# HGRN2 and sliding-window trunk on one core: order of casts, copies and turns at six places, and the last tile in column halves

## The chip, the cores and the metric

The kernel runs on one core of a Trainium2 chip. The metric is the time of one execution on the device, in microseconds (us). Before the change the median of three timed runs is 2102.97 us (2102.83 to 2103.01).

## What is computed

The input `x` has 1024 tokens of 1024 features, in float32. Two layers follow, each a token mixer and a gated feed-forward network (FFN), every one of the four sub-layers closed by a layer norm of `ALPHA * h + sublayer(h)`:

```python
# layer 0: HGRN2, 8 heads of 128
q, f, i, g = jnp.split(h @ w_in, 4, axis=-1)                  # w_in: 1024 x 4096
fg = lb + (1.0 - lb) * jax.nn.sigmoid(heads(f))               # lb: softmax over two rows of logits
o = hgrn2_chunkwise(jax.nn.silu(heads(q)), 1.0 - fg, heads(i), jnp.log(fg))
o = o * lax.rsqrt(jnp.mean(jnp.square(o), -1, keepdims=True) + RMS_EPS)
o = o * g_norm_w * jax.nn.silu(heads(g))
mix = o.reshape(B, S, D) @ w_out
# S_t = diag(f_t) S_{t-1} + k_t v_t^T ;  o_t = S_t^T q_t
# layer 1: attention over a window of 128, 16 query heads and 4 shared key/value heads, with sinks and a bias
# each layer's FFN, 1024 -> 2 x 2816 -> 1024:
u = causal_depthwise_conv3(h @ w_in) + conv_b
a, b = jnp.split(u, 2, axis=-1)
ff = (jax.nn.silu(a) * b) @ w_out
h = layer_norm(ALPHA * h + ff, g, b)
```

## The kernel before

**Products.** A float32 product is made of three matmuls of a reduced format, fp32r. Each operand is split into a *high* part, its cast to fp32r, and a *low* part, the operand less its high part. `mm3` (L222 to L224) issues high by high, high by low and low by high into one PSUM bank. `split` (L249) makes both parts: the high one is a cast on ScalarE (ACT), the low one a subtraction on VectorE (DVE) in `low_part` (L197). So each operand passes through ScalarE and then VectorE before TensorE (PE) can finish with it. `T` holds the turned (transposed) activations, features on the partitions: `T[:, 0]` is the high part, `T[:, 1]` the low. `HL` holds the split weights. `psmm` are PSUM tiles of one bank (128 x 512), `psax` PSUM tiles of two banks (128 x 1024).

**What sets the order.** Most of the program is under a manual schedule: each engine executes its instructions in the order in which the Python code emits them, and an object `od` interleaves the emission. `od.t` is a planned time in us that the code of TensorE's products moves on; `od.spawn(task, delay)` and `od.later(delay, call)` put a task aside until the plan has come that far, `yield d` in a task waits for d planned us, `od.behind(x, y)` works out such a wait from how far VectorE's own plan is ahead, and `od.tick()`, called after each k step of three matmuls, emits what is due. A delay therefore only chooses the place in the engines' orders. While the chip runs, an instruction waits for its operands and for whatever stands ahead of it on its engine.

**The beginning.** `x` arrives in eight blocks of 128 tokens in `Y`, and the weights of head 0's values and gates in two pieces, `raw0` and `raw1`, on the SP queue. TensorE first runs matmuls on a zero tile `still`. `x_block(0)` transposes block 0 into two banks, casts them, makes the low parts and copies the rows out to `xf[0]` (the tile `St`, L923). `ig_second` (L840) splits `raw1`; `first_rows` (L851) multiplies blocks 0 and 1 by both pieces. `x_first` turns block 1 (again by `x_block`, its rows go to `qp`) and blocks 2 and 3 (`turn_block`, a `psax` tile; the rows go to `tot` and `og`, L965). In all of them the low part is made from PSUM. `lower_bounds` (`le`, L976 to L978) runs between block 2 and block 3 on ScalarE. `ig_block` (L811 and L812) then multiplies blocks 2 and 3, and blocks 4 to 7 are turned by `x_pair`, which also spawns `sums_of_x`, sums of blocks for the later products by block schemes.

**Head 0.** `first_qf` makes the forget gate and the query of head 0. `forget` makes the gate of a half of the tokens by three activations on ScalarE (L1041, L1045, L1046), which give `fg` and `kp`. `recur` is the recurrence of one head; its first operation on VectorE is `qp = qs * fg` (L1158).

**The other heads.** Their q, f, i and g projections are made by 7-product block schemes (`line` lists them), with `evacuate` taking each product out of PSUM. A head's last value product is followed by `turn_values` (its transposes are in the group L232, the copy back is L1254, the waited-for copy L1421). `norm` closes a head: squares, a scale on VectorE (L1275), the transposes of `og`, and for the last head the split of the result into `T`. The results of heads 0 to 6 come back and are split into `T` by `move`, which puts the low parts into the list `moved_lows`; `lay`, called while ticking, takes from it what is due, and `lay_all` the rest. The out-projection `out_pass` (L1574) reads them.

**FFN.** `Up.run` multiplies by a 7-product scheme: column block after column block (`fc`) of two weight columns. Its first products, before all blocks of the normed activations are there, are run in parts: of product 1, for fc 0 and 1, the columns of three token blocks first, then `make` finishes the sums (`TX`, `rx`), then the fourth, 128 columns wide. `collect` takes products out of PSUM: product 1 is copied twice by ScalarE (L522, L523), the others are added by VectorE. `Down` runs seven products, the last of which is number 4, and `evacuate` (L691) adds each bank to `Y`. After product 4's tile `tb` follow `ln_half` (statistics of 512 columns, L263), then `ln_affine`: `ln_stats` aggregates (L269, L270, and a power on GpSimd), two passes scale (L280, L283), and the rows leave on the SP queue.

Of the kernel before, what the change touches and what calls it, by code (L numbers as in the profile page):

```python
# [134 lines left out]
def trunk(ctx: ExitStack, tc: tile.TileContext, a: dict, out: bass.AP):  # L135
# [120 lines left out]

    half_stats = {}

    def ln_half(tb, i):

        if tb not in half_stats:
            half_stats[tb] = sm.tile([P, 2, 6], F32, name="st", bufs=8)
        nc.vector.bn_stats(half_stats[tb][:, i, :], Y[:, tb, i * 512:(i + 1) * 512])  # L263

    def ln_stats(tb):
        st = half_stats.pop(tb)
# [28 lines left out]
    def quarters(to, rows):  # L295
# [110 lines left out]
    class Up:  # L406
# [93 lines left out]
            split(blocks(1, 0), blocks(1, 1), r1)  # L500
            split(blocks(2, 0), blocks(2, 1), r2)

        def product(self, p, fc, ps, cols=slice(0, 512)):
# [9 lines left out]
            for k in range(4):  # L513
# [55 lines left out]
        def run(self, ready, down):  # L569

            od.finish(ready[:4])
            tiles = [psax(), psax()]
            ax = [tiles[i % 2][:, i // 2 * 512:(i // 2 + 1) * 512] for i in range(4)]

            for (p, fc), ps in zip([(p, fc) for p in (4, 5) for fc in range(2)], ax):
                self.product(p, fc, ps)
            self.make(ready[4:], 1)
            mm = [psmm() for _ in range(4)]
            self.pairs = [mm, ax]
            firsts = list(zip([(p, fc) for p in (1, 2) for fc in range(2)], mm))  # L580
            if self.l == 0:
                for (p, fc), ps in firsts[:2]:
                    self.product(p, fc, ps, slice(0, 3 * P))
            for part in range(2, 5):
                self.make(ready[4:], part)
            if self.l == 0:
                for (p, fc), ps in firsts[:2]:
                    self.collect(p, fc, self.product(p, fc, ps, slice(3 * P, 4 * P)))
                firsts = firsts[2:]
            for (p, fc), ps in firsts:  # L590
                self.collect(p, fc, self.product(p, fc, ps))
            for fc in range(2):
                self.collect(6, fc, self.product(6, fc, mm[fc]))
            for fc in range(2):
                self.collect(7, fc, self.product(7, fc, mm[2 + fc]))
                self.collect(4, fc, ax[fc])
                self.collect(5, fc, ax[2 + fc])
            self.weights(2)
            for fc in range(2):
                self.collect(3, fc, self.product(3, fc, mm[fc]))  # L600
            banks, n = mm[2:] + ax[:2] + mm[:2] + ax[2:], 0
            for fc in range(2, NF):
                if fc > 2:
                    self.weights(fc)
                for p in (1, 2, 6, 7, 4, 5, 3):
                    self.collect(p, fc, self.product(p, fc, banks[n % 8]))
                    n += 1
                    if fc == NF - 1 and p in (1, 6, 4):
                        down.ahead.append(down.operands(0, len(down.ahead)))

    class Down:
# [70 lines left out]
        def evacuate(self, p, tb, ps, ln):  # L682
# [7 lines left out]
                else:  # L690
                    tt(y, y, ps, op=op)  # L691

            if p in (2, 3, 4, 7):
                ln_half(tb if p in (2, 3) else tb + 4, 0 if p in (2, 4) else 1)
            if p in (3, 4):
                task = ln(tb if p == 3 else tb + 4, self)
                if task is not None:
                    self.tasks.append(od.spawn(task))

        def product(self, i, ln):  # L700
            p, H = self.ORDER[i], self.H
# [6 lines left out]
            for k, tb in steps + [(k, tb) for tb in range(4) for k in range(late, H)]:  # L708
                if k not in hls:
                    hls[k] = self.operands(i, k)  # L710
                hl = hls[k]
                mm3(banks[tb], lambda j: hl[:, j, 0, tb * P:(tb + 1) * P], lambda j: hl[:, j, 1, :],
                    k == 0, k == H - 1)
                od.tick()
                if k == H - 1:
                    if i < 2:
# [33 lines left out]
    with tc.tile_pool(name="t", bufs=1, reuse_waits="tile") as raws, hgrn_pool as hp:  # L750
# [157 lines left out]
        with tc.tile_pool(name="ep", bufs=1, reuse_waits="tile") as ep:  # L908
# [5 lines left out]
            def x_block(tb):  # L914
                ts = slice(tb * P, (tb + 1) * P)
                halves = [psmm() for _ in range(2)]
                for k in range(KC):
                    tr(halves[k // 4][:, k % 4 * P:(k % 4 + 1) * P], Y[:, tb, k * P:(k + 1) * P])
                for i, ps in enumerate(halves):
# [22 lines left out]
            with tc.manual_schedule(engines={EN.PE, EN.SP, EN.Activation, EN.DVE}):  # L942
# [8 lines left out]
                le = ep.tile([P, 2, NH], F32, name="le")  # L951

                idle = psmm()
                for n in (9, 3):
                    for _ in range(n):
                        nc.tensor.matmul(idle[:, :P], still, still, start=True, stop=True)
                    if n == 9:
                        x_block(0)
                us.append(ig_second(raw1))

                def x_first():
                    x_block(1)
                    yield 1.0
                    for tb in (2, 3):
                        nc.scalar.copy(xf[tb], turn_block(tb, False))  # L965
                        if tb == 2:
                            yield 1.2

# [89 lines left out]
        def first_qf(weights):  # L1058

            qs, fg, kp = weights["out"] = head_tiles()  # L1060
            for half in range(2):
# [10 lines left out]
                nc.scalar.activation(qs[:, ts], ps, AF.Silu)  # L1072
# [1 line left out]
        def recur(h, qs, fg, kp):  # L1074
# [183 lines left out]
        def norm(h, pv):  # L1258
# [145 lines left out]
        def evacuate(m, p, ps, taken):  # L1404
# [14 lines left out]
                nc.scalar.copy(second[:, late], ps)  # L1419
            elif p == 4 and g:  # L1420
                nc.scalar.copy(first[:, late], ps)  # L1421
# [531 lines left out]
```

## Time and profile before

| | before |
|---|---|
| median of three timed runs | 2102.97 us (2102.83 to 2103.01) |
| the profiled execution | 2104.41 us |
| its span in the profile | 2102.6 us |
| granted TensorE clock | 0.999 |
| TensorE busy | 2083.4 us (99%) |
| VectorE busy | 1773.6 us (84%) |
| ScalarE busy | 970.3 us (46%) |
| GpSimd busy | 174.9 us (8%) |
| DMA, mean | 136 GB/s |

How to read the rows quoted below. Times count from the start of the span, in us. A row of a timeline gives the start, how long the instruction or group of instructions was busy, the engine, the line, the operation with its output and inputs by the names in the program, sizes (partitions x elements), and a count. Brackets at the end hold the time in which the engine stood idle just before, and which instruction on which engine ended that wait. A row of the waits gives the waiting group, the group it waited for, and the total, the number and the longest of these waits. Ends of matmuls are modelled, so matmuls that overlap in the pipeline can show times that overlap. The lines are those of the kernel before.

### The profile page before, as it was taken

What the parts mean: (1) busy time and instruction counts of PE and PEld (TensorE: products, weight loads), DVE (VectorE), ACT (ScalarE), POOL (GpSimd) and SP (SyncE); (2) the same over time, 40 slices, a digit from 0 to 9 for tenths busy, and PEclk for the clock granted to TensorE, in tenths of its full rate; (3) what the DMA queues carried; (4) which work ended last, traced back from release to release, by engine and by line L of the source; (5) the groups of instructions that cost most, each with busy time, mean ns of one, the idle gap of its engine ahead of it and who ended that gap; (6) DMA issues with size and microseconds to landing.
All of it is one profiled execution on the core that took longest, in us unless ns stands there. A gap on an engine that the chain in (4) does not pass through costs nothing.

```text
span 2102.6 us, 31643 instructions
## 1 busy us (share of the span) xinstructions
PE 2083.4 (99%) x12327; PEld 1737.3 (83%) x12327; DVE 1773.6 (84%) x2432; ACT 970.3 (46%) x1588; POOL 174.9 (8%) x210
## 2 busy tenths in 40 slices
PE   9999999999999999999999999999999999999998
PEld 7878888878888888888888888888888888888886
DVE  6778788769999999887977678979999999978986
ACT  6555555633444444444433367733544444444430
POOL 1000000001000000000001123312000010000002
PEclk9999999999999999999999999999999999999999
DMA  4111111333256866538755411051266676459662
GB/s 154 41 51 51 51 52 51 130 107 120 91 138 178 193 169 154 141 120 300 245 180 180 131 36 47 14 179 71 91 169 183 165 191 153 111 168 327 211 216 95
DMA packets 239823, 286.82 MB, mean 136 GB/s; under 512 B 30216, under 2 KB 160440, under 8 KB 239416
## 3 DMA queue, kind: packets, MB, share of 16 engines
q1 hardware_dynamic: 223360, 238.26, 35.1%
q0 software_dynamic: 15456, 46.16, 10.9%
q8 instruction: 97, 1.59, 0.3%
q14 instruction: 54, 0.44, 0.1%
q10 hardware_dynamic: 856, 0.37, 0.1%
HBM read 241.72 MB, written 89.15 MB: 157 GB/s over the span
## 4 chain that ended last, share of the span: by engine, by line
PE 89%; DVE 6%; ACT 2%; DMA 2%; issue 1%; SPq 0%; POOL 0%; DVEq 0%; ACTq 0%; POOLq 0%
PE psmm L222 17%; PE psmm L223 17%; PE psmm L224 17%; PE psax L222 9%; PE psax L223 9%; PE psax L224 9%; PE psax L228 3%; PE psmm L228 1%; PE psax L1727 1%; PE psax L232 1%; PE psmm L232 1%; DVE HL L197 1%; DMA rx<-in_ffn_w_in_dram 1%; PE psmm L1574 1%; DVE T L197 1%
## 5 line engine op out<-in xcount | busy, mean ns | idle before, releaser
L222 PE MATMUL psmm<-T,HL 128*128 128x512 f32 (+1 forms) x824 | 324.3, 394 | 1.0 <-DVE VG L1431 0.8
L223 PE MATMUL psmm<-T,HL 128*128 128x512 f32 (+1 forms) x824 | 319.8, 388 | 1.5 <-DVE T L197 1.5
L224 PE MATMUL psmm<-T,HL 128*128 128x512 f32 (+1 forms) x824 | 319.9, 388 | 0.2 <-DVE HL L197 0.2
L544 DVE SCALAR_TENSOR_TENSOR Y<-Y,cwt,Y 128x1023 f32<-128x1023 f32 (+1 forms) x176 | 225.1, 1280 | 46.7 <-ACT Y L542 45.4
L249 ACT CAST HL<-rx 128x1024 fp32r<-128x1024 f32 (+1 forms) x151 | 151.3, 1005 | 162.7 <-PE psmm L223 25.5
L197 DVE TENSOR_TENSOR HL<-rx,HL 128x1024 fp32r<-128x1024 f32 (+1 forms) x151 | 174.5, 1161 | 19.5 <-ACT HL L249 19.1
L222 PEld LDWEIGHTS psmm<-T,HL 128*128 128x128 f32 x824 | 154.7, 188 | 32.8 <-issue 1.3
L224 PEld LDWEIGHTS psmm<-T,HL 128*128 128x128 f32 x824 | 154.8, 188 | 32.6 <-DVE HL L197 0.6
L223 PEld LDWEIGHTS psmm<-T,HL 128*128 128x128 f32 x824 | 154.9, 188 | 32.3 <-DVE T L197 2.2
L222 PE MATMUL psax<-T,HL 128*128 128x512 f32 x392 | 152.9, 390 | 0.3 <-ACT Y L523 0.3
L223 PE MATMUL psax<-T,HL 128*128 128x512 f32 x392 | 152.6, 389 | 0.0
L224 PE MATMUL psax<-T,HL 128*128 128x512 f32 x392 | 152.5, 389 | 0.0
L542 ACT ACTIVATE Y<-Y,cwt 128x1024 f32<-128x1024 f32 x88 | 108.8, 1237 | 84.0 <-DVE Y L531 82.5
L197 DVE TENSOR_TENSOR HL<-raw,HL 128x512 fp32r<-128x512 f32 (+1 forms) x121 | 92.1, 787 | 30.6 <-ACT HL L1334 21.0
L271 POOL TENSOR_TENSOR rs<-rs,nhalf 128x1 f32<-128x1 f32 x32 | 45.6, 1427 | 737.9 <-DVE rs L270 737.9
L249 ACT CAST HT<-rx 128x1024 fp32r<-128x1024 f32 (+1 forms) x37 | 35.5, 961 | 135.0 <-DVE rx L498 64.9
L222 PEld LDWEIGHTS psax<-T,HL 128*128 128x128 f32 x392 | 73.7, 188 | 16.1 <-ACT Y L523 0.7
L222 PE MATMUL psmm<-HL 128*128 128x512 f32 x220 | 86.7, 394 | 0.0
L224 PEld LDWEIGHTS psax<-T,HL 128*128 128x128 f32 x392 | 73.5, 188 | 15.3
L223 PEld LDWEIGHTS psax<-T,HL 128*128 128x128 f32 x392 | 73.6, 188 | 15.1
L224 PE MATMUL psmm<-HL 128*128 128x512 f32 x220 | 85.8, 390 | 0.0
L223 PE MATMUL psmm<-HL 128*128 128x512 f32 x220 | 85.6, 389 | 0.0
(407 smaller groups left out, 5179.9 us busy)
## 6 DMA issues: line engine op xcount, KB each, us to landing
rx<-in_ffn_w_in_dram SPq DMA_DIRECT2D x136, 256.0 KB
rx<-gd SPq DMA_DIRECT2D x118, 256.0 KB
bsd<-in_ffn_w_out_dram POOLq DMA_DIRECT2D x36, 768.0 KB, 8.3
gd<-Y SPq DMA_DIRECT2D x44, 512.0 KB
raw<-in_hgrn_w_in_dram SPq DMA_DIRECT2D x30, 512.0 KB
rx<-in_ffn_w_out_dram SPq DMA_DIRECT2D x54, 256.0 KB
R<-bsd SPq DMA_DIRECT2D x44, 256.0 KB
Y<-in_ffn_w_in_dram SPq DMA_DIRECT2D x40, 256.0 KB
```

The lines of the kernel that those rows point to most:

```text
L197: make = lambda e: e.tensor_tensor(lo, src, hi.bitcast(F32), op=ALU.subtract)
L222: nc.tensor.matmul(ps, st(0), mv(0), start=start, stop=False, skip_group_check=onto)
L223: nc.tensor.matmul(ps, st(0), mv(1), start=False, stop=False, skip_group_check=onto)
L224: nc.tensor.matmul(ps, st(1), mv(0), start=False, stop=stop, skip_group_check=onto)
L228: nc.tensor.matmul(ps, lhsT, rhs, start=start, stop=stop, **kw)
L232: nc.tensor.transpose(ps, src, ident)
L249: nc.scalar.copy(hi, src)
L271: nc.gpsimd.tensor_tensor(rs, rs, nhalf, op=ALU.pow)
L542: nc.scalar.activation(c, u, AF.Identity, bias=cwt[:, l, 3, ci:ci + 1], scale=cwt[:, l, 2, ci:ci + 1])
L544: nc.vector.scalar_tensor_tensor(c[:, sh:], u[:, :S - sh], cwt[:, l, 2 - sh, ci:ci + 1], c[:, sh:], op0=ALU.mult, op1=ALU.add)
L1574: nc.tensor.matmul(ps, T[:, x, kc, tb * P:(tb + 1) * P], us[kc][:, w, :], start=start and kc == 0, stop=False)
L1727: nc.tensor.matmul(self.pv[:, e, jj, lo:], self.q[bp // 2][es, e, qs], Kl[es, pp, ks] if low else Kh[:, pp, e, ks], start=not low and jj = ...
```

## The change

1. *Beginning.* Eight matmuls on the zero tile stand ahead of block 0's transposes, not nine. ScalarE casts `raw1` after the casts of block 0 and copies block 0's rows behind that (`x_block(0)` hands the copies back to be called later). For blocks 1, 2 and 3 the low part is made from the copy in SBUF and no longer from PSUM.
2. *First gate later.* For the first half of the tokens `forget` is put 2.5 planned us later.
3. *Turn of values.* `turn_values` is spawned after 4.0 instead of 3.0 planned us for heads 1 and 2.
4. *Moved heads' lows.* In the last head's recurrence, up to two entries of `moved_lows` are called behind the copy of `kd`.
5. *Last output's turn.* In the last head's `norm` the wait ahead of the transposes is `od.behind(0.0, 1.4)` instead of `od.behind(1.2, 2.4)`.
6. *First products of the first up-projection.* The two 128-column products first run high by high and low of the weights by high of the activations, for both `fc` (16 matmuls), then high of the weights by low of the activations (8); both are collected after that.
7. *Last tile in column halves.* In the last layer the last tile of product 4 runs its last two k steps for 256 columns, adds and takes statistics of these, and then the same for the other 256 (`Down.end`). The statistics of that row block are then in four parts.

ScalarE at the beginning. `T` is the turned `x`, `raw_113` the second weight piece, and `St`, `qp`, `tot` and `og` the rows of blocks 0 to 3. Before:

```order
L249 CAST T<-psmm 128x4x128 x2
L923 COPY St<-psmm 128x512 x2
L840 CAST HL<-raw_113 128x512 x2
L249 CAST T<-psmm 128x4x128 x2
L923 COPY qp<-psmm 128x512 x2
L249 CAST T<-psax 128x8x128
L965 COPY tot<-psax 128x1024
L977 ACTIVATE le<-le 128x16
```

And now:

```order
L960 CAST T<-psmm 128x4x128 x2
L873 CAST HL<-raw_113 128x512 x2
L956 COPY St<-psmm 128x512 x2
L960 CAST T<-psmm 128x4x128 x2
L956 COPY qp<-psmm 128x512 x2
L294 CAST T<-psax 128x8x128
L295 COPY tot<-psax 128x1024
L1023 ACTIVATE le<-le 128x16
```

The casts of the weight piece have changed places with the copies of block 0; from there on ScalarE's order is the old one, but VectorE's lows of blocks 1 to 3 now read what the copies write.

ScalarE around the first gate. `fg` and `kp` are head 0's gate, `qs` its query, and the casts into `T` are those of blocks 6 and 7. Before:

```order
L889 CAST Y_309<-kd 128x4x128
L1041 ACTIVATE fg<-psmm 128x512
L1045 ACTIVATE fg<-fg,lbt 128x512
L1046 ACTIVATE kp<-fg,one 128x512
L249 CAST T<-psax 128x8x128 x2
L1072 ACTIVATE qs<-psmm 128x512
```

And now:

```order
L922 CAST Y_308<-kd 128x4x128
L249 CAST T<-psax 128x8x128 x2
L1087 ACTIVATE fg<-psmm 128x512
L1091 ACTIVATE fg<-fg,lbt 128x512
L1092 ACTIVATE kp<-fg,one 128x512
L1121 ACTIVATE qs<-psmm 128x512
```

The casts of blocks 6 and 7 have moved ahead of the gate's three activations.

ScalarE at the first up-projection. `TX` is made of sums of the normed activations in `Y` and `rx`, and the copies L522 and L523 (now L532 and L533) take the first product of each `fc` out of PSUM. Before:

```order
L249 CAST TX<-Y_4187 128x4x128
L522 COPY Y_4187<-psmm 128x512
L249 CAST TX<-Y_4187 128x4x128
L523 COPY Y_4187<-psmm 128x512
L249 CAST TX<-rx_4709 128x4x128
L249 CAST TX<-rx_4711 128x4x128
L522 COPY Y_4187<-psmm 128x512
L523 COPY Y_4187<-psmm 128x512
```

And now:

```order
L249 CAST TX<-Y_4186 128x4x128 x2
L249 CAST TX<-rx_4708 128x4x128
L532 COPY Y_4186<-psmm 128x512
L533 COPY Y_4186<-psmm 128x512
L249 CAST TX<-rx_4710 128x4x128
L532 COPY Y_4186<-psmm 128x512
L533 COPY Y_4186<-psmm 128x512
```

The first product's copies now stand behind the third cast. Elsewhere: on TensorE the transposes of heads 1 and 2's values come one k step of three matmuls later, those of the last output one k step sooner; ahead of head 1's copy L1254 ScalarE takes one Silu (L1436); VectorE's order around the moved lows is the same row for row; at the end VectorE alternates additions and statistics of 256 columns, and the first matmul of the second half waits for VectorE's first addition. The orders of GpSimd and of SP are unchanged.

The diff, cut to what is spoken of here:

```diff
-    def turn_block(tb, spread):
+    def turn_block(tb, spread, kept=None):
...
-        split(T[:, 0, :, ts], T[:, 1, :, ts], ps.rearrange("p (k t) -> p k t", k=KC))
+        if kept is not None:
+            nc.scalar.copy(T[:, 0, :, ts], ps.rearrange("p (k t) -> p k t", k=KC))
+            nc.scalar.copy(kept, ps)
+            low_part(T[:, 1, :, ts], kept.rearrange("p (k t) -> p k t", k=KC), T[:, 0, :, ts], None)
+        else:
+            split(T[:, 0, :, ts], T[:, 1, :, ts], ps.rearrange("p (k t) -> p k t", k=KC))
...
+            for n in range(0 if part is None else 4):
+                for i, j in ((0, 0), (1, 0)) if part == 0 else ((0, 1),):
+                    nc.tensor.matmul(ps[:, cols], fixed(i, n), moving(j, n)[:, cols], start=part == 0 and n == i == 0,
+                                     stop=part == 1 and n == 3)
...
             if self.l == 0:
+                for part in range(2):
+                    for (p, fc), ps in firsts[:2]:
+                        self.product(p, fc, ps, slice(3 * P, 4 * P), part)
+                od.t += 24 * P / 2365.0
+                od.tick()
                 for (p, fc), ps in firsts[:2]:
-                    self.collect(p, fc, self.product(p, fc, ps, slice(3 * P, 4 * P)))
+                    self.collect(p, fc, ps)
...
+        def end(self, ps, hls, ln):
+            for half in range(2):
+                cols = slice(256 * half, 256 * half + 256)
+                for k in hls:
+                    hl = hls[k]
+                    mm3(ps[:, cols], lambda j: hl[:, j, 0, 3 * P:4 * P], lambda j: hl[:, j, 1, cols], False,
+                        k == self.H - 1, n=256, onto=True)
+                tt(Y[:, 7, cols], Y[:, 7, cols], ps[:, cols], op=add)
+                ln_half(7, half, 4)
+            ln(7, self)
...
                 for i, ps in enumerate(halves):
                     ks = slice(4 * i, 4 * i + 4)
-                    split(T[:, 0, ks, ts], T[:, 1, ks, ts], ps.rearrange("p (k t) -> p k t", k=4))
-                for i, ps in enumerate(halves):
-                    nc.scalar.copy(xf[tb][:, 512 * i:512 * i + 512], ps)
+                    nc.scalar.copy(T[:, 0, ks, ts], turned(ps))
+                    if tb == 0:
+                        low_part(T[:, 1, ks, ts], turned(ps), T[:, 0, ks, ts], None)
+                if tb == 0:
+                    return copies
+                copies()
+                for i in range(2):
+                    ks = slice(4 * i, 4 * i + 4)
+                    low_part(T[:, 1, ks, ts], turned(xf[tb][:, 512 * i:512 * i + 512]), T[:, 0, ks, ts], None)
...
                 us.append(ig_second(raw1))
+                copies()
...
-                        nc.scalar.copy(xf[tb], turn_block(tb, False))
+                        turn_block(tb, False, xf[tb])
...
-                forget(0, fg, kp, ts, ps)
+                if half:
+                    forget(0, fg, kp, ts, ps)
+                else:
+                    od.later(2.5, lambda ts=ts, ps=ps: forget(0, fg, kp, ts, ps))
...
             nc.scalar.copy(kd, ps)
+            if h == NH - 1:
+                for _ in range(min(2, len(moved_lows))):
+                    moved_lows.pop(0)[1]()
...
-            yield od.behind(1.2, 2.4 if h == NH - 1 else 3.4)
+            yield od.behind(0.0, 1.4) if h == NH - 1 else od.behind(1.2, 3.4)
...
-                od.spawn(turn_values(h), 3.0)
+                od.spawn(turn_values(h), 4.0 if h < 3 else 3.0)
```

More of the change, by code (lines that the diff above doesn't have):

```diff
@@ L257, in trunk, with ln_half @@
     half_stats = {}
[L259 removed]
+    def ln_half(tb, i, parts=2):
         if tb not in half_stats:
[L262 to L263 removed]
+            half_stats[tb] = sm.tile([P, parts, 6], F32, name=f"st{parts}", bufs=8 if parts == 2 else 1)
+        n = D // parts
+        nc.vector.bn_stats(half_stats[tb][:, i, :], Y[:, tb, i * n:(i + 1) * n])
     def ln_stats(tb):
@@ L501, in weight_sums, with product @@
             split(blocks(2, 0), blocks(2, 1), r2)
-        def product(self, p, fc, ps, cols=slice(0, 512)):
+        def product(self, p, fc, ps, cols=slice(0, 512), part=None):
             TX = self.TX
@@ L691, in evacuate @@
                     tt(y, y, ps, op=op)
-            if p in (2, 3, 4, 7):
+            if self.last and tb == 3 and p == 7:
+                for i in (2, 3):
+                    ln_half(7, i, 4)
+            elif p in (2, 3, 4, 7):
                 ln_half(tb if p in (2, 3) else tb + 4, 0 if p in (2, 4) else 1)
@@ L711, in product @@
                 hl = hls[k]
+                if self.last and p == 4 and tb == 3 and k >= H - 2:
+                    if k == H - 1:
+                        self.end(banks[tb], {n: hls[n] for n in (H - 2, H - 1)}, ln)
+                    continue
                 mm3(banks[tb], lambda j: hl[:, j, 0, tb * P:(tb + 1) * P], lambda j: hl[:, j, 1, :],
-                    k == 0, k == H - 1)
+                    k == 0, k == H - 1 or self.last and p == 4 and tb == 3 and k == H - 3)
                 od.tick()
@@ L918, in x_block, with copies @@
                     tr(halves[k // 4][:, k % 4 * P:(k % 4 + 1) * P], Y[:, tb, k * P:(k + 1) * P])
+                turned = lambda t: t.rearrange("p (k t) -> p k t", k=4)
+                def copies():
+                    for i, ps in enumerate(halves):
+                        nc.scalar.copy(xf[tb][:, 512 * i:512 * i + 512], ps)
                 for i, ps in enumerate(halves):
                     ks = slice(4 * i, 4 * i + 4)
-                    split(T[:, 0, ks, ts], T[:, 1, ks, ts], ps.rearrange("p (k t) -> p k t", k=4))
-                for i, ps in enumerate(halves):
-                    nc.scalar.copy(xf[tb][:, 512 * i:512 * i + 512], ps)
+                    nc.scalar.copy(T[:, 0, ks, ts], turned(ps))
[7 more added lines that the diff above has]
+                    low_part(T[:, 1, ks, ts], turned(xf[tb][:, 512 * i:512 * i + 512]), T[:, 0, ks, ts], None)
             def x_pair(tb):
```

8 lines of the change are left out of this document (4 added, 4 removed).

## The prediction

> **What bounds the kernel now.** I read the page first, then the waits of TensorE, and then, around each wait, the timeline of TensorE (PE), ScalarE (ACT) and VectorE (DVE). The page gives the busy times:
>
> ```profile
> PE 2083.4 (99%) x12327; PEld 1737.3 (83%) x12327; DVE 1773.6 (84%) x2432; ACT 970.3 (46%) x1588; POOL 174.9 (8%) x210
> ```
>
> TensorE is busy all but 19 of 2102.6 us, so a change that removes no matmuls can only shorten its few waits and the tail behind its last matmul. The waits of TensorE, the two longest groups (total, times, longest):
>
> ```profile
> PE psmm L223 <- DVE T L197: 1.5, 2, 0.9
> PE psmm L1574 <- DVE T L197: 1.2, 1, 1.2
> ```
>
> Every place that the change touches is one of those waits or the tail. The tail, from TensorE's and VectorE's timeline:
>
> ```profile
> 2093.67 0.39 PE L223 MATMUL psmm<-HL 128*128 128x512 f32 x1
> 2093.90 0.39 PE L224 MATMUL psmm<-HL 128*128 128x512 f32 x1
> 2094.33 0.69 DVE L691 TENSOR_TENSOR Y<-Y,psmm 128x512 f32<-128x512 f32 x1 [2.71 <-PE psmm L224]
> 2095.05 0.69 DVE L263 BATCH_NORM_STATS2 st<-Y 128x6 f32<-128x512 f32 x1
> 2095.78 0.21 DVE L269 BATCH_NORM_AGGREGATE mv<-st 128x2 f32<-128x12 f32 x1
> ```
>
> Two matmuls stand 0.23 apart, though each is modelled as 0.39 long. So an idle time shown in brackets hides another 0.16: what a wait of a full matmul costs is its bracket plus 0.16. I count that way throughout.
>
> **The beginning: casts ahead of copies, lows from copies.** TensorE, ScalarE and VectorE, each from its own timeline:
>
> ```profile
> 9.92 1.50 PE L851 MATMUL psmm<-HL,T 128*128 128x256 f32 x8 [0.99 <-ACT HL L840]
> 22.28 0.39 PE L812 MATMUL psmm<-HL,T 128*128 128x256 f32 x1
> 23.33 1.09 PE L232 MATMUL psax<-ident,Y 128*128 128x128 f32 x8 [0.66 <-ACT og L965]
> ```
>
> ```profile
> 9.24 1.14 ACT L840 CAST HL<-raw 128x512 fp32r<-128x512 f32 x2
> 15.11 1.01 ACT L249 CAST T<-psax 128x1024 fp32r<-128x1024 f32 x1 [0.70 <-PE psax L232]
> 17.42 1.01 ACT L965 COPY tot<-psax 128x1024 f32<-128x1024 f32 x1 [1.29 <-DVE T L197]
> 18.33 0.22 ACT L977 ACTIVATE le<-le 128x16 f32<-128x16 f32 x1
> 19.97 1.00 ACT L249 CAST T<-psax 128x1024 fp32r<-128x1024 f32 x1
> 22.26 1.01 ACT L965 COPY og<-psax 128x1024 f32<-128x1024 f32 x1 [1.29 <-DVE T L197]
> ```
>
> ```profile
> 16.16 1.23 DVE L197 TENSOR_TENSOR T<-psax,T 128x1024 fp32r<-128x1024 f32 x1 [2.37 <-ACT T L249]
> 17.70 0.24 DVE L976 TENSOR_TENSOR le<-par,lm 128x8 f32<-128x8 f32 x2
> ```
>
> The cast at 9.24 now stands ahead of the row copies, so TensorE resumes earlier by s. How much depends on when the second weight piece lands, which no row shows. s lies between 0 (it lands just at 9.24) and the 0.99 that TensorE idles; I take the middle, 0.5. Everything up to block 2's turn then runs s earlier. From there the new order has a price. ScalarE casts block 2 at 15.11 - s and copies it one step of 0.91 later (18.33 less 17.42), until 17.03 - s. The low part, made from the copy now, starts at 17.07 - s and not at 16.16. The lower bounds' input `le` is ready 1.78 after that low's start (17.70 + 0.24 - 16.16), at 18.85 - s, and the Exp waits for it: before, it merely stood behind the copy, at 18.33. So block 3's cast goes from 19.97 to 20.49 - s, its copy ends 0.91 + 1.01 later at 22.41 - s, and its low, 1.23 long, ends at 23.68 - s. The matmul that reads this low ran at 22.28; now it waits until 23.73 - s, and block 5's transposes, the next instruction, start 0.12 behind it: 23.85 - s against 23.33. The term is 0.52 - s: **0.0**, from -0.5 to +0.5. The waits at 9.92 and 23.33 go, and one for block 3's low takes their place. Dropping one warm-up matmul costs nothing, since TensorE waits for weights behind it in any case.
>
> **First gate later.** The places, TensorE, ScalarE, VectorE:
>
> ```profile
> 32.97 0.50 PE L224 MATMUL psmm<-T,HL 128*128 128x512 f32 x1 [0.17 <-DVE HL L197]
> 41.14 0.50 PE L223 MATMUL psmm<-T,HL 128*128 128x512 f32 x1 [0.91 <-DVE T L197]
> ```
>
> ```profile
> 34.33 0.59 ACT L1041 ACTIVATE fg<-psmm 128x512 f32<-128x512 f32 x1
> 36.50 1.91 ACT L249 CAST T<-psax 128x1024 fp32r<-128x1024 f32 x2
> ```
>
> ```profile
> 37.53 1.23 DVE L197 TENSOR_TENSOR T<-psax,T 128x1024 fp32r<-128x1024 f32 x1 [1.23 <-ACT T L249]
> 39.87 1.22 DVE L197 TENSOR_TENSOR T<-psax,T 128x1024 fp32r<-128x1024 f32 x1
> ```
>
> The copy of block 3 ends at 21.9 (22.41 - s) where it ended at 23.27, so the casts behind it and VectorE's lows run about 1 us ahead; that covers the wait at 32.97, which cost 0.17 + 0.16 = 0.33. With the gate's three activations moved behind the casts of blocks 6 and 7, VectorE no longer idles the 1.23 ahead of 37.53. Block 7's low, which ended at 41.09, ends about 1.1 + 1.2 earlier, at 38.8. TensorE gets to it at 41.14 - 1.07 - 0.33 = 39.7, so the wait of 0.91 + 0.16 = 1.07 goes with 0.9 to spare. Term: **-1.4**, from -1.5 to -1.0. The gate itself ends some 2 us later; its results are first read by head 0's recurrence, at 57.20 (below).
>
> **Turn of the values of heads 1 and 2.** One k step of three matmuls, 3 x 0.23 = 0.68, is now issued ahead of the transposes that wait for ScalarE:
>
> ```profile
> 122.53 0.66 PE L232 MATMUL psax<-ident,VG 128*128 128x128 f32 x4 [0.82 <-ACT VG L1421]
> 173.43 0.66 PE L232 MATMUL psax<-ident,VG 128*128 128x128 f32 x4 [0.36 <-ACT VG L1421]
> ```
>
> They cost 0.82 + 0.16 = 0.98 and 0.36 + 0.16 = 0.52; 0.68 and 0.52 of that are filled. Term: **-1.2**, from -1.2 to -0.6. In head 1 ScalarE now takes one Silu ahead of the copy of the turned values; the row at 122.53 is no reader of that copy, and costs nothing more.
>
> **Moved heads' lows.** The wait that they are made for:
>
> ```profile
> 443.64 2.56 PE L1574 MATMUL psmm<-HL,T 128*128 128x512 f32 x10 [1.19 <-DVE T L197]
> 442.90 0.68 DVE L197 TENSOR_TENSOR T<-VG,T 128x512 fp32r<-128x512 f32 x1
> ```
>
> The low that TensorE waits for is that of head 6 (`VG`), the fourth in the list; the change calls the first two, and VectorE had these ahead of the states' chain already. Its order there stays as it was, row for row. Term: **0**.
>
> **Last output's turn.** The turn is issued one k step (0.68) sooner, and the chain of ScalarE and VectorE behind it with it:
>
> ```profile
> 463.74 0.50 PE L222 MATMUL psmm<-HL,T 128*128 128x512 f32 x1 [1.01 <-ACT T L249]
> ```
>
> The wait of 1.01 + 0.16 = 1.17 shrinks by 0.68. Term: **-0.7**, from -0.7 to -0.4.
>
> **First products of the first up-projection** (the column block 3, 128 wide). TensorE, then ScalarE:
>
> ```profile
> 546.16 0.33 PE L223 MATMUL psmm<-T,HL 128*128 128x128 f32 x1 [0.62 <-DVE T L197]
> 554.32 0.39 PE L222 MATMUL psmm<-TX,HT 128*128 128x512 f32 x1
> ```
>
> ```profile
> 552.77 0.62 ACT L249 CAST TX<-rx 128x512 fp32r<-128x512 f32 x1
> 553.97 0.63 ACT L249 CAST TX<-rx 128x512 fp32r<-128x512 f32 x1 [0.58 <-DVE rx L458]
> 554.50 0.57 ACT L522 COPY Y<-psmm 128x512 f32<-128x512 f32 x1
> 554.97 0.59 ACT L523 COPY Y<-psmm 128x512 f32<-128x512 f32 x1
> ```
>
> The 16 matmuls that need no low part go first, so the wait at 546.16 goes: about 0.7. But both products now end together, and ScalarE takes the first product's two copies behind the cast at 552.77 rather than around the one before. Copies follow a cast 0.53 and 1.00 later (553.97 to 554.50 and 554.97), so the second ends at 552.77 + 1.00 + 0.59 = 554.36. The product at 554.32 writes the bank that they read: it would come 0.7 sooner, and waits until 554.4 instead. The gain is given back: **+0.1**, from -0.7 (if VectorE, which feeds these casts, is that much sooner) to +0.3.
>
> **Last tile in column halves.** Half a matmul is taken as 0.12, half of the 0.23. For VectorE's half:
>
> ```profile
> 28.05 0.41 DVE L784 TENSOR_TENSOR VG<-VG,psmm 128x256 f32<-128x256 f32 x1
> ```
>
> Six half matmuls from 2092.77 (five steps of 0.23 ahead of 2093.90) end at about 2093.64; VectorE adds until 2094.09. The second half's six lie in the same PSUM bank, and the first of them waits for that addition. It starts at 2094.14; six take 0.7, the last's pipeline 0.16 and the restart 0.1: 2095.10. Then addition and statistics, 0.41 + 0.45: the aggregate starts at 2096.05 instead of 2095.78. Term: **+0.3**. Were the halves to overlap, TensorE would end at 2094.3, the second addition at 2094.9, and the aggregate would start at 2095.4: -0.4.
>
> [...]
>
> **Sum.** 0.0 - 1.4 - 1.2 + 0 - 0.7 + 0.1 + 0.3 = **-2.9**. The profiled execution took 2104.41 (span 2102.6 and 1.8 around it) and would take 2101.5. The three timed runs are 1.4 below it, with a median of 2102.97: 2100.1. That is 0.14%; a measurement of this kernel tells about 0.2% (4.2 us) from no change.
>
> **Rivals.** (1) *VectorE and ScalarE set the pace* (slower). TensorE has more waits for their chain, and would only wait longer there:
>
> ```profile
> 63.68 0.50 PE L222 MATMUL psmm<-T,HL 128*128 128x512 f32 x1 [0.28 <-DVE VG L784]
> 52.15 0.60 ACT L1072 ACTIVATE qs<-psmm 128x512 f32<-128x512 f32 x1 [1.16 <-PE psmm L224]
> 57.20 1.22 DVE L1158 TENSOR_TENSOR qp<-qs,fg 128x1024 f32<-128x1024 f32 x1
> ```
>
> It decides at 57.20: if head 0's first step doesn't start sooner, the gate's 1.4 is given back at 63.68, and likewise the 1.2 and 0.7 at the next waits for the heads' chain. What stays is +0.4: 2103.4. For it speaks VectorE's 84%; against it, that the chain into 57.20 starts with the activation at 52.15, which waits for TensorE, so it moves along. (2) *Only the beginning is given back*, at 63.68, for the same reason: -1.5, 2101.5. (3) *All goes as the edits' names say*: no new waits for block 3's low, for the copies at 554, or between the halves: -1.3 more at the start (s and the 0.66 + 0.16 at 23.33), -0.8 and -0.7 more at the other two, so -5.7: 2097.3. Against it stand the chains worked out above. That an edit doesn't do what it says holds for the moved lows, and is in the sum.
>
> **Chances.** Forecast 0.72, its own range 2098.9 to 2101.4 from the terms' bounds; (1) 0.07; (2) 0.12; (3) 0.09. The range reaches to (2) and half-way to (3): 2098.3 to 2102.0. Faster by over 0.2% means below 2098.8: (3) and the edge of the forecast, 0.13. Slower by over 0.2% would need more than any case gives: 0.02. Within 0.2%: 0.85.
>
> **What would show it.** Right: no wait at 9.92 and 23.33, one of about 1.7 ahead of the matmul at 22.28 for `og`'s low; none at 32.97 and 41.14; about 0.3 left at 122.53 and none at 173.43; the wait at 443.64 as long as before; about 0.5 left at 463.74; none at 546, about 0.7 at 554; and at the end TensorE pausing some 0.5 between the halves. Wrong: a longer wait at 63.68 or 113 (rivals 1 and 2), block 3's low ready in time, or the second half starting before the first addition ends (rival 3).

## The result, and the profile after

The change made the kernel slower: 2114.65 us (2114.04 to 2116.61, four runs) against 2102.99 (2102.83 to 2104.34), a ratio of 1.0056 (95% interval 1.0038 to 1.0073). The forecast was 2100.1, within 2098.3 to 2102.0. The profiled execution spans 2112.9 us where it spanned 2102.6.

The waits of TensorE do not show it. The page of after and the waits of after, longest groups first (total, times, longest):

```profile
PE 2096.8 (99%) x12331; PEld 1738.4 (82%) x12331; DVE 1776.7 (84%) x2435; ACT 970.0 (46%) x1588; POOL 175.4 (8%) x210
```

```profile
PE psmm L845 <- DVE T L197: 1.5, 1, 1.5
PE psmm L1626 <- DVE T L197: 1.2, 1, 1.2
...
PE psmm L884 <- ACT HL L873: 0.9, 1, 0.9
```

TensorE's *busy* time grew by 13.4 us, with four more matmuls in its records. Its idle time in the span fell, from 19.2 us (2102.6 - 2083.4) to 16.1 (2112.9 - 2096.8); the matmuls themselves take longer. TensorE's timeline of after tells where it begins:

```profile
440.82 2.58 PE L1626 MATMUL psmm<-HL,T 128*128 128x512 f32 x10 [1.19 <-DVE T L197]
460.22 0.51 PE L222 MATMUL psmm<-HL,T 128*128 128x512 f32 x1 [0.31 <-ACT T L249]
```

These two stood at 443.64 and 463.74. So behind the last output's turn TensorE was 3.5 us ahead, where the forecast's terms up to there add to -3.3. What was lost was lost after it, without a wait: the last tile's half matmuls start where six whole ones stood, and they start 9.9 us later. Before (TensorE's timeline):

```profile
2092.77 0.39 PE L222 MATMUL psmm<-HL 128*128 128x512 f32 x1
```

And after:

```profile
2102.66 0.28 PE L222 MATMUL psmm<-HL 128*128 128x256 f32 x1
...
2104.05 0.39 PE L222 MATMUL psmm<-HL 128*128 128x256 f32 x1 [0.51 <-DVE Y L725]
```

Now the groups of TensorE between 1450 and 1850 us, in the second up-projection, each shape apart (busy time, mean ns of one). Before:

```profile
L223 PE MATMUL psmm<-TX,HL 128*128 128x512 f32 x52 | 20.2, 389 | 0.0
L223 PE MATMUL psmm<-TX,HT 128*128 128x512 f32 x36 | 14.0, 389 | 0.0
```

And after:

```profile
L223 PE MATMUL psmm<-TX,HL 128*128 128x512 f32 x48 | 19.1, 398 | 0.0
L223 PE MATMUL psmm<-TX,HT 128*128 128x512 f32 x36 | 14.2, 394 | 0.0
```

The same matmul, 512 columns of `TX` against weights in `HL`, takes 9 ns more. The modelled length follows the distance of the starts: 0.227 us from one to the next before, 0.234 to 0.235 now (means of L222 to L224), over two up-projections of over 400 us each. The diff touches nothing there, but for the first products at 546. What it touches is memory: the statistics in four parts are a tile of their own, 96 bytes in every partition, and the program allocates it ahead of all tiles that come and go. The addresses of the compiled programs, in bytes within a partition:

```
            T      HL       HT (weights)  TX       T2
before      4096   102400   152576        177152   209920
after       4096   102400   152672        177248   210016
```

Before, all of these are multiples of 256. Now the last three stand 96 further, and `T` and `HL` stay.

### The profile page after: what moved, and what is told of

Its sections match the earlier page's. It is cut to its first block, busy times and chain, and to the rows that moved or that the text cites. A ratio compares the mean times of both kernels' runs of the same rounds, so it can differ in the third digit from the quotient of the medians.

```text
span 2112.9 us, 31654 instructions
## 1 busy us (share of the span) xinstructions
PE 2096.8 (99%) x12331; PEld 1738.4 (82%) x12331; DVE 1776.7 (84%) x2435; ACT 970.0 (46%) x1588; POOL 175.4 (8%) x210
## 4 chain that ended last, share of the span: by engine, by line
PE 96%; DVE 2%; ACT 1%; DMA 0%; issue 0%; SPq 0%; DVEq 0%; ACTq 0%
PE psmm L222 19%; PE psmm L224 19%; PE psmm L223 19%; PE psax L223 10%; PE psax L224 10%; PE psax L222 10%; PE psax L228 3%; PE psmm L232 1%; PE psmm L228 1%; PE psax L232 1%; PE psax L1779 1%; PE psmm L1626 1%; DMA raw<-in_hgrn_w_in_dram 0%; DVE HL L197 0%; ACT HL L1386 0%
## 5 line engine op out<-in xcount | busy, mean ns | idle before, releaser
L222 PE MATMUL psmm<-T,HL 128*128 128x512 f32 (+1 forms) x816 | 322.7, 395 | 1.1 <-DVE VG L1483 0.8
L223 PE MATMUL psmm<-T,HL 128*128 128x512 f32 (+1 forms) x816 | 318.8, 391 | 0.0
L224 PE MATMUL psmm<-T,HL 128*128 128x512 f32 (+1 forms) x816 | 318.5, 390 | 0.0
L222 PEld LDWEIGHTS psmm<-T,HL 128*128 128x128 f32 x816 | 153.4, 188 | 34.2 <-issue 1.3
L224 PEld LDWEIGHTS psmm<-T,HL 128*128 128x128 f32 x816 | 153.3, 188 | 32.5
L223 PEld LDWEIGHTS psmm<-T,HL 128*128 128x128 f32 x816 | 153.4, 188 | 31.0
L223 PE MATMUL psax<-T,HL 128*128 128x512 f32 x392 | 153.7, 392 | 0.0
L222 PE MATMUL psax<-T,HL 128*128 128x512 f32 x392 | 153.4, 391 | 0.0
L224 PE MATMUL psax<-T,HL 128*128 128x512 f32 x392 | 153.4, 391 | 0.0
L222 PE MATMUL psmm<-HL 128*128 128x512 f32 (+1 forms) x222 | 87.2, 393 | 0.5 <-DVE Y L725 0.5
L222 PEld LDWEIGHTS psax<-T,HL 128*128 128x128 f32 x392 | 73.7, 188 | 16.3
L223 PEld LDWEIGHTS psax<-T,HL 128*128 128x128 f32 x392 | 73.6, 188 | 16.3
L224 PEld LDWEIGHTS psax<-T,HL 128*128 128x128 f32 x392 | 73.6, 188 | 15.8
L224 PE MATMUL psmm<-HL 128*128 128x512 f32 (+1 forms) x222 | 86.4, 389 | 0.0
L223 PE MATMUL psmm<-HL 128*128 128x512 f32 (+1 forms) x222 | 86.3, 389 | 0.0
```

The source lines that it names most:

```text
L222: nc.tensor.matmul(ps, st(0), mv(0), start=start, stop=False, skip_group_check=onto)
L223: nc.tensor.matmul(ps, st(0), mv(1), start=False, stop=False, skip_group_check=onto)
L224: nc.tensor.matmul(ps, st(1), mv(0), start=False, stop=stop, skip_group_check=onto)
```

## The experiments

**Addresses or order.** Two theories: the shift of 96 bytes slows the matmuls (address theory), or the moved casts, copies and halves load other engines or DMAs so that they do (order theory). An unused tile moves all that follow it and adds no instruction. In the kernel before and in the kernel after:

```diff
     rim = sp.tile([P, 32], F32, name="rim")
+    pad = sp.tile([P, N], F32, name="pad")   # N = 24, 16, 8 in before; 8 in after
```

> The kernel before, with 96 bytes left unused behind the small tiles and nothing else: same instructions in the same order, later tiles 96 bytes further. Address theory: 2115 to 2118 us, with matmuls from TX at 0.232 to 0.236 us apart and no new waits. Order theory: 2103.

> The same with 64 bytes. Address theory: if TensorE reads in lines of 64 bytes, 2103; if in lines of 128 bytes, as slow as with 96 (2115 to 2118). Order theory: 2103.

> The same with 32 bytes. Address theory: with lines of 64 or 128 bytes 2115 to 2118; if only some multiple of 32 matters, 2103. Order theory: 2103.

> The kernel after, with 32 bytes per partition left unused behind the small tiles, so that the new statistics tile (96 bytes) moves all later tiles by 128 bytes instead of 96. Same instructions. Address theory (tiles that start 96 bytes past a multiple of 128 are read more slowly by TensorE): the pace of 0.227 us a matmul is back in both up-projections, and the time is 2099 to 2101 us, near the forecast's sum. Rival, order theory (the moved casts, copies and column halves load VectorE, ScalarE or the DMA queues so that matmuls run slower): stays at 2114 to 2115.

| kernel | later tiles moved by | median us | ratio to before (95%) |
|---|---|---|---|
| b_pad96 | 96 | 2117.76 | 1.0071 (1.0057 to 1.0085) |
| b_pad64 | 64 | 2111.73 | 1.0041 (1.0027 to 1.0055) |
| b_pad32 | 32 | 2114.46 | 1.0055 (1.0042 to 1.0069) |
| a_pad32 | 96 + 32 = 128 | 2107.91 | 1.0023 (1.0014 to 1.0033) |

before: 2103.09. The order theory fell: the old instructions in the old order are 14.7 us slower by a shift of 96 bytes alone. Beside that kernel, which has the same addresses, the changed one is 3.1 us faster, and the forecast was -2.9. But my address theory, with lines of 64 or 128 bytes, fell as well: 64 and 128 are slow too, at 2111.7 and 2107.9, between the cases written down for them. In a_pad32 one group told more, in the same window as above (the added line moves the three matmuls of `mm3` to L223 to L225):

```profile
L223 PE MATMUL psmm<-TX,HL 128*128 128x512 f32 x52 | 20.5, 395 | 0.0
L223 PE MATMUL psmm<-TX,HT 128*128 128x512 f32 x36 | 14.1, 390 | 0.0
```

`TX` is slow against `HL`, which did not move, and nearly as fast as ever against `HT`, which moved with it. So it looked like the distance between the two operands.

**Matmuls alone.** One moving tile and one stationary tile, no other engine at work behind the first 10 us and no DMA of note behind 20, 36 matmuls a line in the up-projection's pattern:

> Only matmuls of the up-projection's pattern (fp32r, 128x512 moving, stationary blocks of 128 columns in turn, 36 of them a line), from tiles of zeros, with no other engine at work; it leaves all else out and writes zeros. Each line has another start of the moving tile (0 to 2048 bytes past a multiple of 4096) and of the stationary tile (0 to 1024). If only the moving tile's start counts (a line of 64 or 128 bytes read twice), the pace depends on the moving start alone: 0.227 us at multiples of 128, 0.232 to 0.236 at 32, 64 and 96 past one. If the two reads of TensorE collide (theory of the pair), it depends on the difference of both starts: equal starts are fast whatever they are. If other engines or DMAs make the delay (theory of contention), all lines run at 0.227.

TensorE's timeline (L82: both starts 0; L83 to L85: moving start 32, 64, 96; L118: both 96; L119: moving 128, stationary 96):

```profile
14.01 8.32 PE L82 MATMUL ps<-M,W 128*128 128x512 f32 x36
22.17 8.57 PE L83 MATMUL ps<-M,W 128*128 128x512 f32 x36
30.58 8.41 PE L84 MATMUL ps<-M,W 128*128 128x512 f32 x36
38.83 8.57 PE L85 MATMUL ps<-M,W 128*128 128x512 f32 x36
...
314.18 8.35 PE L118 MATMUL ps<-M,W 128*128 128x512 f32 x36
322.36 8.57 PE L119 MATMUL ps<-M,W 128*128 128x512 f32 x36
```

From L82's start to L83's are 8.16 us, 226.7 ns a matmul; from L83's to L84's 8.41, 233.6. In ns a matmul, from the starts in the trace, without the first three matmuls of each line, which can still be slowed by the line before:

```
stationary   moving start
start        0      32     64     96     128    192    256    512    1024
0            226.7  233.3  228.8  233.7  233.3  233.3  226.7  226.7  226.7
32           233.3  226.7  233.3  228.8  233.7  234.3  233.3  233.3  233.3
64           233.3  233.3  227.0  233.3  228.8  232.6  233.3  233.3  233.3
96           234.4  233.3  233.3  227.0  233.3  233.4  234.4  234.3  234.2
128          233.3  234.4  233.3  233.3  227.0  228.9  232.1  232.2  232.4
256          227.3  233.3  228.8  233.7  233.3  233.3  226.7  226.7  226.7
```

The fast entries (226.7 to 227.3) are those in which both starts agree modulo 256 bytes, whichever of the starts in the table they are; a moving start 64 further costs 2 ns, the other multiples of 32 cost 5 to 8, most of them 6.6. No other engine and no DMA is needed for it: between 30 and 650 us VectorE and ScalarE are not busy at all, and the busy share of the DMA engines rounds to 0.00. Neither address is slow by itself (227.0 with both at 96, 233.7 and 234.4 with one of them at 96 and the other at 0): the pair is.

**In the kernel: 256 bytes, and all alike.** Three kernels, beside a before of 2103.27. The first has 160 unused bytes behind the 96 of the new tile (`N = 40` in the kernel after). The second has the last tile whole again, so that there is no new tile. The third has 96 bytes ahead of `T`, so that every operand moves alike:

```diff
+    pad = cp.tile([P, 24], F32, name="pad")
     T = cp.tile([P, 2, KC, S], F32R, name="T")
```

> The kernel after with 160 unused bytes behind the small tiles, so that the later tiles stand 256 bytes further than before the change. Same instructions. Theory of the pair, as the run of matmuls alone showed it (fast where the starts of the moving and the stationary tile agree modulo 256 bytes): all tiles agree again, matmuls 0.227 us apart in both up-projections, time 2099 to 2100.5 us, the forecast's sum of about -3. Rival (a page of 1024 or 2048 bytes matters): 2107 to 2112, as with 128.

> The kernel after with its last tile whole again, as before: no column halves, and so no tile for statistics in four parts and no shift. Theory of the pair: 2099 to 2101 us; beside the run with 160 bytes it prices the halves, forecast at +0.3 and seen in the profile after as about -0.5. Rival (an edit in the beginning or the middle is what slows the matmuls): 2112 to 2115.

> The kernel before with 96 unused bytes ahead of T, so that T, Y, HL and every pool tile behind them start 96 bytes further, all alike. Theory of the pair: all differences are as before, so 2103 us, with the pace of 0.227. Theory of a line of 128 bytes (each tile's own start counts): slower than the 2118 of the run that shifted the later tiles alone, since now every operand of every product is off.

| kernel | median us | ratio to before (95%) |
|---|---|---|
| a_pad160 | 2100.52 | 0.9987 (0.9978 to 0.9997) |
| a_whole | 2099.27 | 0.9983 (0.9974 to 0.9992) |
| b_pad96_all | 2104.47 | 1.0006 (0.9996 to 1.0015) |

The theory of the pair held three times. The groups again, a_pad160 and then b_pad96_all:

```profile
L223 PE MATMUL psmm<-TX,HL 128*128 128x512 f32 x52 | 20.2, 389 | 0.0
...
L223 PE MATMUL psmm<-TX,HT 128*128 128x512 f32 x40 | 15.6, 389 | 0.0
```

```profile
L223 PE MATMUL psmm<-TX,HL 128*128 128x512 f32 x52 | 20.2, 389 | 0.0
...
L223 PE MATMUL psmm<-TX,HT 128*128 128x512 f32 x36 | 14.0, 389 | 0.0
```

With 96 bytes everywhere none of these operands starts at a multiple of 64, and the pace is the old one. a_whole and a_pad160 differ by the halves and by less than their spread (1.25 us, with runs of each over more than 3): the medians do not price the halves, the timeline does, below, and there the "about -0.5" of the expectation does not come out.

**The other side of the pair.** The kernel before with `HL` alone moved, by 96:

```diff
+    pad0 = cp.tile([P, 24], F32, name="pad0")
     HL = cp.tile([P, 12, 1024], F32R, name="HL")
...
     rim = sp.tile([P, 32], F32, name="rim")
+    pad = sp.tile([P, 40], F32, name="pad")
```

> The kernel before with 96 unused bytes ahead of HL and 160 behind the small tiles, so that HL alone differs from all others by 96 bytes modulo 256. Theory of the pair: every product with HL's weights on one side and T, TX or T2 on the other is now off, some 5500 matmuls of 512 columns at 0.006 to 0.008 us more: 2135 to 2148 us. Theory that only the moving operand's start counts: 2103 to 2106, since HL is mostly stationary.

2137.84 us against 2102.41, 1.0166 (1.0146 to 1.0186): 35.4 us, where the pair gave 32 to 45. `T` (in the rows `T2` bears that name too, since numbers are left out) is slow against `HL` now, and fast against `HT`, which stands where it did modulo 256 (the same window):

```profile
L224 PE MATMUL psmm<-T,HL 128*128 128x512 f32 x174 | 68.9, 396 | 0.0
...
L224 PE MATMUL psmm<-T,HT 128*128 128x512 f32 x20 | 7.8, 389 | 0.0
```

**How it slows.** A second run of matmuls alone, with shorter loads and shorter reads:

> Matmuls alone again, on tiles of zeros, all else left out: the moving start at 0 to 256 bytes in steps of 32 and at 4 and 16, the stationary start at 0; then stationary blocks of 64 and 32 columns, moving blocks of 256 and 128 columns, and one stationary block over and over, each at distances of 0, 64 and 96 bytes. If the weight load of one matmul and the moving read of the one before it get in each other's way, the extra time of a 512-column matmul (6.6 ns at 96 bytes) is about halved with 64 stationary columns and quartered with 32, and is the same with 256 moving columns. If the moving read itself is slowed for as long as the distance is wrong, the extra goes with the moving columns (3.3 ns at 256, 1.7 at 128) and not with the stationary ones. Between multiples of 32, 4 and 16 bytes: as slow as 32 in either case.

In ns a matmul, without the first five of each line, at distances of 0, 64 and 96 bytes:

```
                                  0      64     96
stationary 128, moving 512        226.7  228.9  233.5
stationary 64, moving 512         230.0  228.6  231.5
stationary 32, moving 512         231.7  231.6  233.3
stationary 128, moving 256        120.0  117.8  120.0
stationary 128, moving 128        111.6  111.6  111.6
one stationary block throughout   227.4  228.9  233.7
```

Distances of 4 and 16 cost 11.2 and 4.9, and 160 and 224 cost 7.8 and 6.6. Both of my accounts of the mechanism fell. Shorter stationary blocks do not shrink the loss, they take the fast case away; at 256 moving columns a distance of 64 is the fast one, and at 128 all are alike. So "equal modulo 256" was the fast case of full blocks alone, 128 stationary columns and 512 moving ones (226.7 against 228.9 and 233.5). How the pair slows the matmul stays open.

**The edits one by one.** The kernel before with the later gate alone, and with the new beginning alone:

> The kernel before with the first gate later and nothing else. Theory (each wait is worth its bracket plus 0.16): the wait of 0.91 at 41.14 goes and TensorE stands 1.0 us sooner from there on, beyond 63.68 and 95 too: 2102 us. Rival (given back where the heads' chain is waited for): the wait at 63.68 grows from 0.3 to over 1 and TensorE is no sooner behind it: 2103.

> The kernel before with the new beginning alone (warm-up, casts ahead of copies, lows of blocks 1 to 3 from the copies). Theory: the waits at 9.92 and 23.33 shrink and one of about 1.5 us for block 3's low comes ahead of 23; TensorE stands 0.0 to 0.7 us sooner at 26, and the wait of 0.17 at 32.97 goes as well: 2102 to 2103 us. Rival (the new order at the beginning is a gain of 1.5 as its name says): TensorE 1.5 us sooner at 26.

Medians of 2101.43 (0.9995, 0.9985 to 1.0004) and 2101.01 (0.9994, 0.9985 to 1.0004) beside 2102.41: not told from no change, as expected. The waits of TensorE between 5 and 66 us say more, first b_gate, then b_start:

```profile
PE psmm L851 <- ACT HL L840: 0.9, 1, 0.9
PE psax L232 <- ACT og L965: 0.7, 1, 0.7
PE psmm L222 <- DVE VG L784: 0.3, 1, 0.3
PE psmm L224 <- DVE HL L197: 0.2, 1, 0.2
```

```profile
PE psmm L833 <- DVE T L197: 1.4, 1, 1.4
PE psmm L872 <- ACT HL L861: 0.3, 1, 0.3
PE psmm L222 <- DVE VG L805: 0.3, 1, 0.3
PE psmm L872 <- DVE HL L852: 0.3, 1, 0.3
```

The wait of 0.9 for `T` at 41.14 is in neither. Each edit removes it alone, so it must not be credited to both; and the wait of 0.2 at 32.97 goes with the beginning, not with the gate. The wait of 0.3 for `VG`, at 63.68 before, stays what it was in both: nothing was given back there.

**A version that is faster than both.** From a_pad160: the low of block 2 behind the preparation of the lower bounds on VectorE, and up to four moved lows instead of two.

```diff
-                for _ in range(min(2, len(moved_lows))):
+                for _ in range(min(4, len(moved_lows))):
...
+                    held.pop()()                    # block 2's low_part, kept back by turn_block
                     nc.scalar.activation(le, le, AF.Exp)
```

> The kernel after with 160 unused bytes, and two things made to do what they were meant to: the low of block 2 stands behind the preparation of the lower bounds on VectorE, so that Exp and block 3's cast come sooner and the wait of 1.5 us for block 3's low goes; and up to four moved lows, not two, are made ahead of the states' chain, so that head 6's low is among them and the wait of 1.2 us at the out-projection goes. Expected 2096.5 to 2098 us if nothing takes their place; 2099 to 2100 if the gains are given back at later waits.

2095.20 us, 0.9962 (0.9949 to 0.9975) of before: 8.1 us less, and some 1.3 below what was expected. Exp no longer waits, so block 3's cast and its low come 1.4 us sooner (VectorE's timeline; the low stood at 21.73 in after), and TensorE does not wait at 22.00:

```profile
16.00 0.24 DVE L1026 TENSOR_TENSOR le<-par,lm 128x8 f32<-128x8 f32 x2
16.91 1.23 DVE L198 TENSOR_TENSOR T<-tot,T 128x1024 fp32r<-128x1024 f32 x1 [0.67 <-ACT tot L296]
...
20.36 1.23 DVE L198 TENSOR_TENSOR T<-og,T 128x1024 fp32r<-128x1024 f32 x1 [1.29 <-ACT og L296]
```

Its waits between 66 and 560 us no longer hold the one for `T` at the out-projection; one of the forecast's has come at the first up-projection instead:

```profile
PE psmm L223 <- ACT Y L535: 0.8, 1, 0.8
PE psmm L223 <- DVE VG L1488: 0.8, 2, 0.4
```

## Why the prediction was wrong

**The step that failed** is the pricing of "Last tile in column halves": "Half a matmul is taken as 0.12 ... Term: +0.3". It priced the instructions and left out what the edit allocates. Behind it stands the premise that such a change "can only shorten its few waits and the tail": the pace of the matmuls in between, 0.23, was taken as fixed. Nowhere did the working ask where the tiles stand, and so "Slower by over 0.2% would need more than any case gives" was wrong: the case was missing. Its price is 14.7 us by b_pad96, and 14.1 by the kernel after less a_pad160.

With the addresses put right, the sum comes out: a_pad160 is 2.75 us below its before (0.6 to 4.6 by its interval), against -2.9. So close an agreement is in part luck, since some terms were right for another reason than was given, and two waits, for the second weight piece and at 546, differ from one execution to the next. The forecast's own range is not what the terms' bounds add up to, either: plain addition gives 2098.0 to 2102.1. Point by point:

- *Beginning, 0.0:* right in kind. The waits at 9.92 and 23.33 were to give way to one for block 3's low "of about 1.7" (bracket and 0.16); after shows 1.5 + 0.16. The wait for the second weight piece did not go: TensorE arrives sooner and still waits 0.9 (0.3 in b_start). By ScalarE's row below its cast waits for the DMA, so the piece's landing ends it, and that differs from one execution to the next (the cast starts at 8.51 here, at 7.88 in b_start): behind it TensorE stood 0.76 sooner at 26 in b_start, but 0.65 sooner in b_gate too, which has the old beginning. What is left for the order itself is about 0.1, less than these executions can tell.

```profile
8.51 1.14 ACT L873 CAST HL<-raw 128x512 fp32r<-128x512 f32 x2 [1.72 <-DMA raw<-in_hgrn_w_in_dram]
```

- *Gate, -1.4:* the sum of both waits was right, the owner wrong. The beginning alone removes both (in b_start TensorE gains 1.4 between 26 and 42), the gate alone only the larger (1.2 in b_gate). In after a wait of 0.42 for `kp` of head 0's chain, at 81.48, takes 0.4 of it back; a_pad160, with the same instructions, does not have it.
- *Turns, -1.2:* in after's waits between 66 and 560 us the group for `VG` from ScalarE, 1.2 us before, is gone; no wait over 0.2 stands at either place. The row at 122.53 was to keep about 0.3 and kept none.
- *Moved lows, 0:* right. The wait is 1.2 as before; with four lows instead of two it goes (a_best), so the number of lows called was what kept the edit from working.
- *Last output's turn, -0.7:* the wait of 1.01 is 0.31. Right.
- *First products, +0.1:* not settled. The wait of 0.62 at 546 is absent in after, but also in b_gate and b_start, which have the old code there: that row changed from one execution to the next. The wait for ScalarE's second copy that was to replace it does not show in after, and shows in a_best with 0.8.
- *Column halves, +0.3:* as instructions, right. From the start of the last six (or twelve half) matmuls to the aggregate it was 2095.78 - 2092.77 = 3.01; now, by VectorE's row below and the start at 2102.66, it is 3.32. The second half waits for the first addition in the same bank, 0.51 in the row at 2104.05 above, as the forecast had it.

```profile
2103.57 0.42 DVE L725 TENSOR_TENSOR Y<-Y,psmm 128x256 f32<-128x256 f32 x1 [2.06 <-PE psmm L224]
...
2105.98 0.26 DVE L270 BATCH_NORM_AGGREGATE mv<-st 128x2 f32<-128x24 f32 x1
```

- *Rivals:* none was it. Rival 1, the only slow one, was to decide at 57.20 by the chain behind `qs`; in after that activation starts 1.8 us sooner, at 50.36, and head 0's first step as much sooner, at 55.41 (VectorE's row below). The wait that stood at 63.68 stays 0.3, so rival 2 did not come true either. Rival 3 had no new waits for block 3's low and between the halves, and after has both.

```profile
55.41 1.22 DVE L1207 TENSOR_TENSOR qp<-qs,fg 128x1024 f32<-128x1024 f32 x1
```

## What to carry to other kernels

A new tile is an edit to every tile allocated behind it: before pricing a change by its instructions, compare the addresses of both programs, and keep the operands of the large matmuls equal modulo 256 bytes (pad a new small tile, as a_pad160 does: 2100.52 us where the kernel after took 2114.65; allocating it behind the large ones should do as well, but was not run). When a kernel is slower and no wait has grown, compare the mean length of one matmul, shape by shape, before looking for a cause among engines. And a wait that two edits can each remove is worth its price once.

## What the runs showed of the hardware

In both runs of matmuls alone the pace of a 128x512 fp32r matmul went with the distance of its operands' starts: 226.7 to 227.3 ns where they agree modulo 256 bytes, 228.8 or 228.9 with the moving start 64 further, 232 to 235 at other multiples of 32, and 237.9 at 4.

Behind a product with the wrong distance the right ones were slow too, for a while: against `HT`, which moved with it, `TX` still takes 394 ns in after and 389 in before. The starts in the trace show it fade: of the twelve matmuls of such a product in after, the first three start 235 ns apart on average and the last three 228. The matmuls alone show it too, with no other engine at work: in L92 of the first run, a matched line behind a mismatched one, the first seven starts are 225 to 240 ns apart, and from then on all are 226 or 227.

In a_pad32, at 128 bytes, that trailing loss is nearly gone (390). It goes with this that the shift of 128 cost 7.4 us (a_pad32 less a_pad160) and that of 32 cost 11.4, though both cost 6.6 ns a matmul alone; that it is the whole of the difference was not worked out, and why it trails is open.
